# PSUM column order in a hybrid decoder layer: sums kept in the order in which the products read their columns, put back into token order by the evictions

## The chip, the cores and the metric

The kernel runs on one core of one Trainium2 chip. The metric is the device time of one execution in microseconds; the median of several runs is compared. Beside the timed runs there is one profiled execution, whose span is the time from its first to its last instruction.

## What is computed

One decoder layer on 256 tokens and 16 meta tokens, width 2048, all in float32:

```python
h = concatenate([meta, x])                          # 272 tokens
xn = rmsnorm(h, norm_mix_g)
proj = xn @ w_in                                    # fq fk fv ff | gq gk gv gr ga | gate_fox gate_gla
o_fox = forgetting_attention(fq, fk, fv, ff)        # 8 heads of 128
o_gla = gated_linear_attention(gq, gk, gv, g_log)   # 4 heads, keys 256, values 512, chunks of 64
o_gla = head_rmsnorm(o_gla, gla_norm_g) * silu(gr)
y = sigmoid(gate_fox) * (o_fox @ w_o_fox) + sigmoid(gate_gla) * (o_gla @ w_o_gla)
h = h + y @ w_out
h = h + square(relu(rmsnorm(h, norm_mlp_g) @ w_ff1)) @ w_ff2      # 8192 wide
return rmsnorm(h, final_norm_g)[16:]
```

## The kernel before

Everything lies transposed: features on the 128 partitions, tokens along the columns. Each large product makes 128 output features for all tokens at a time, a chunk: its weight block of 2048x128 floats is loaded in two halves of 512 KB on SyncE's queue (`weight_half`, L108), ScalarE rounds a half to the float32r tile whi (L120), and VectorE makes the remainder wlo (L121). The moving operand was split in the same way before, into a high part and a low part that lie beside each other. Five halves of weights are in flight.

Three helpers make the products. `mac2` (L142) multiplies whi by the high and the low part at once, 512 columns (L143), and adds wlo times the high part, 256 columns, to the first half of the bank (L144); so a finished bank holds a main sum in columns 0 to 255 and a sum to be added to it in columns 256 to 511. `mac3` (L146) does the same for the 272 tokens with meta tokens, where a bank has room for 512 columns alone: its three products (L148, L150, L152) are 272 columns wide and overlap in the bank, shifted by 16 columns. `gemm2` (L154) and `gemm_all` (L163) loop over the 16 blocks of the contraction. The first seven chunks are issued interleaved with the input loads (L358 to L376) by matmuls of their own (L364, L366).

All these products read the moving operand in an order of steps: `steps` (L135) cuts the columns into groups of 16, and reads the first 4 of each group, then the next 4 of each group, and so on, in four passes. Before the change the output in PSUM is addressed with the same `steps`, so that each sum lands at its token's own column.

The sums leave PSUM by evictions. `total` (L178) copies columns 256 to 511 with ScalarE (L181) and adds the main sum on VectorE (L184). `join` (L173) folds the last 16 columns of a `mac3` bank into its first 16. `add_residual` (L869) adds both halves of a bank to the residual ht (L872, L873). The 272-column sums are read directly by VectorE: by `keys` (L520) for the GLA keys, and by L603, L722 and L758 for values and attention keys. `keys` makes two outputs of each key bank: kx, four runs of 64 tokens (L524), and kz, the last 16 tokens written four times (L526). The scores of a GLA head (`scores`, L556; matmuls at L562) read kx, qx and kz.

The order of the work on each engine is set by a list scheduler over the recorded program. PSUM has eight banks, three in the pool pg for the large products and five in px for all else. `later(n, fn)` holds a function back until n more chunks are issued.

In the tail, the last four chunks of the second feed-forward product put the wlo products first (L926, 256 columns, in steps) with an eviction of their own (L927), and then the whi products by halves of 128 tokens (L942), which read their tokens in a row and write them in a row.

Of the kernel before, what the change touches and what calls it, by code (L numbers as in the profile page):

```python
# [65 lines left out]
def trunk(ctx: ExitStack, tc: tile.TileContext, hT, w_small, w_all, consts, w_alpha2, out):  # L66
# [3 lines left out]
    def nm(s):  # L70
        serial[0] += 1
        return f"{s}_{serial[0]}"
# [62 lines left out]
    def steps(ap):  # L135

        return ap.rearrange("p (i a e) -> p a i e", a=4, e=4)

    def row(x):
        return x.rearrange("p o t -> p (o t)")  # L140

    def mac2(ps, hi, lo, x, first, last):  # L142
        nc.tensor.matmul(steps(ps), hi, steps(row(x)), start=first, stop=False)  # L143
        nc.tensor.matmul(steps(ps[:, 0:NT]), lo, steps(x[:, 0, :]), start=False, stop=last)  # L144

    def mac3(ps, hi, lo, k, first, last):  # L146
        if hi is not None:
            nc.tensor.matmul(steps(ps[:, X_LO]), hi, steps(x_lo[:, k]), start=first, stop=False, skip_group_check=True)  # L148
        if lo is not None:
            nc.tensor.matmul(steps(ps[:, 0:NA]), lo, steps(x_hi[:, k]), start=False, stop=last and hi is None, skip_group_check=True)  # L150
        if hi is not None:
            nc.tensor.matmul(steps(ps[:, 0:NA]), hi, steps(x_hi[:, k]), start=False, stop=last, skip_group_check=True)  # L152

    def gemm2(w, x, k0=0, nk=KT, pool=None):  # L154

# [16 lines left out]

    def join(ps):  # L173
        b = tmp.tile([P, NM], F32, tag="join", name=nm("join"))
        nc.scalar.copy(b, ps[:, NA : NA + NM])
        nc.vector.tensor_tensor(ps[:, 0:NM], ps[:, 0:NM], b, op=ALU.add)

    def total(ps, t=None):  # L178

        b = tmp.tile([P, NT], F32, tag="evb", name=nm("evb"))  # L180
        nc.scalar.copy(b, ps[:, NT:512])  # L181
        if t is None:
            t = tmp.tile([P, NT], F32, tag="evt", name=nm("evt"), bufs=4)
        nc.vector.tensor_tensor(t, ps[:, 0:NT], b, op=ALU.add)  # L184
        return t

    def split_to(dst_hi, dst_lo, src):
# [145 lines left out]
    for s in range(KT // 2):  # L333
        if s + 3 < KT // 2:
            with tc.issue_after(load_stage(s + 3, 0).ins):
                load_h(nc.sync, 2 * s + 6, 2)
            last = load_stage(s + 3, 1).ins
        wa, wb = stages[s]
        for kk in range(2):
            k = 2 * s + kk  # L340
            nc.scalar.activation(x_hi[:, k], h[:, k, 0:NA], AF.Identity, scale=gain(0, k))
            nc.vector.scalar_tensor_tensor(x_lo[:, k, 0:NT], h[:, k, NM:NA], gain(0, k),
                                           x_hi[:, k, NM:].bitcast(F32), op0=ALU.mult, op1=ALU.subtract)
            xm = meta[:, k, :]
# [12 lines left out]

        def products(c, k, part):  # L358
            hi, lo = at[c][0][:, k % 2, :], at[c][1][:, k % 2, :]
            ps, st, sp = first_ps[c], k == 0, k == KT - 1  # L360
            if c == NF - 1:
                mac3(ps, hi if part == 0 else None, lo if part else None, k, st, sp and part == 1)
            elif part == 0:
                nc.tensor.matmul(steps(ps), hi, steps(row(x[:, k])), start=st, stop=False)  # L364
            else:
                nc.tensor.matmul(steps(ps[:, 0:NT]), lo, steps(x[:, k, 0]), start=False, stop=sp)  # L366
# [141 lines left out]
    def gla_head(hd, sg, ready=None):  # L508
# [9 lines left out]
        Q0, Q3 = Q1 - C, NT - Q1  # L518

        def keys(i, ps):  # L520
            def four(ap):
                return ap.rearrange("p (g s t) -> p g s t", g=2, s=2)

            nc.vector.tensor_tensor(kx[:, i].rearrange("p g (s t) -> p g s t", t=C)[:, :, 0:3:2, :],  # L524
                                    four(ps[:, 0 : 4 * C]), four(en[:, i, 0 : 4 * C]), op=ALU.mult)
            nc.vector.tensor_tensor(kz[:, i], *(ap.unsqueeze(1).to_broadcast([P, 4, NB])  # L526
                                                for ap in (ps[:, 4 * C : NA], en[:, i, 4 * C :])), op=ALU.mult)

        if ready:
            ps = gemm_all(next_weights())  # L530
# [69 lines left out]
        for i in range(4):  # L600
            ps = gemm_all(next_weights())
            vT = tmp.tile([P, NA], F32, tag="vT", name=nm("vT"))
            nc.vector.tensor_tensor(vT, ps[:, 0:NA], rb, op=ALU.mult)  # L603
            nc.gpsimd.tensor_copy(vg[:, NB * i : NB * (i + 1)], vT[:, 4 * C :])
            later(1, lambda i=i, vT=vT: turn(i, vT))

# [60 lines left out]
        w = small[k // HK][:, k % HK, :]  # L667
        mac3(ps, w, None, k, k == 0, k == KT - 1)
    join(ps)
    nc.scalar.copy(both[0:40], ps[64:104, 0:NA])  # L670
    nc.vector.tensor_tensor(both[0:40], ps[0:40, 0:NA], both[0:40], op=ALU.add)
# [46 lines left out]
    def fox_head(hd):  # L718
        fk = att.tile([P, NA], F32, tag="fk", name=nm("fk"))
        fq = att.tile([P, NT], F32, tag="fq", name=nm("fq"))  # L720
        ps = gemm_all(next_weights())
        nc.vector.tensor_tensor(fk, ps[:, 0:NA], rb, op=ALU.mult)  # L722
# [35 lines left out]
        nc.vector.tensor_tensor(vT, ps[:, 0:NA], rb, op=ALU.mult)  # L758
        va, pa = [], []
        vb = att.tile([P, P], F32, tag="vb", name=nm("vb"))  # L760

# [105 lines left out]
            nc.gpsimd.tensor_tensor(acc, acc, sq, op=ALU.add)  # L867

    def add_residual(j, ps):  # L869
        b = tmp.tile([P, NT], F32, tag="evb", name=nm("evb"))  # L870
        nc.scalar.copy(b, ps[:, NT:512])
        nc.vector.tensor_tensor(ht[:, j, :], ps[:, 0:NT], ht[:, j, :], op=ALU.add)  # L872
        nc.vector.tensor_tensor(ht[:, j, :], ht[:, j, :], b, op=ALU.add)  # L873

    acc2 = gat.tile([P, NT], F32, tag="acc", name="acc2", bufs=1)
    for j in range(KT):
# [45 lines left out]
    for n in range(NL):  # L922
        j, ps = KT - NL + n, bank(pg if n < 3 else px, "ps")
        w = next_weights(whi[:, n])
        for k in range(KT):
            nc.tensor.matmul(steps(ps[:, 0:NT]), w(k)[1], steps(a[:, k, 0, :]), start=(k == 0), stop=(k == KT - 1))  # L926
        nc.vector.tensor_tensor(ht[:, j, :], ps[:, 0:NT], ht[:, j, :], op=ALU.add)  # L927
        ends.append((j, w, ps))

    def half(t0, between, within=None):  # L930
# [142 lines left out]
```

## Time and profile before

| | us |
|---|---|
| median of 3 runs | 1567.56 (1567.43 to 1567.89) |
| profiled execution | 1566.89 |
| its span | 1565.1 |
| TensorE matmul busy | 1553.5 |
| VectorE busy | 1060.0 |
| ScalarE busy | 790.4 |
| GpSimd busy | 128.2 |

The granted TensorE clock was 0.999 of full speed throughout. In the rows, PE is TensorE, DVE VectorE, ACT ScalarE, POOL GpSimd. A row in order of time begins with start and duration in us; a waiting row gives in brackets the idle time before it and what ended it. Matmul durations overlap, because one begins before the one before it has left the array; the time from start to start is what one costs. A row of windows gives from:to, the length, and TensorE's busy time with the number of matmuls.

### The profile page before, as it was taken

The numbers are of one execution on the slowest core, as the hardware profiler recorded it, in microseconds if no ns is written. First come the engines' busy times: TensorE is split into PE (matmuls) and PEld (weight loads), VectorE is DVE, ScalarE is ACT, GpSimd is POOL, SyncE is SP. The second block draws the span as 40 slices with busy tenths as digits, with TensorE's granted clock in tenths as the row PEclk, the third lists the DMA queues.
The fourth block names the chain that finished last, engine by engine and source line by source line (L and its number), as shares of the span: only waits on it lengthen the run. The fifth ranks groups of instructions, "written<-read, shape, count | busy, mean of one in ns | idle before, by whom it ended". The sixth has DMA issues, their size and how long they took to land.

```text
span 1565.1 us, 25427 instructions
## 1 busy us (share of the span) xinstructions
PE 1553.5 (99%) x9812; PEld 1408.5 (90%) x9812; DVE 1060.0 (68%) x1659; ACT 790.4 (50%) x1271; POOL 128.2 (8%) x213
## 2 busy tenths in 40 slices
PE   9999999999999999999999999999999999999997
PEld 8999999999998888888888888888888888888887
DVE  7898857676665555555777876567655776567655
ACT  7666444455555444444555444444444444444563
POOL 6012000011100000000011000000000000000022
PEclk9999999999999999999999999999999999999999
DMA  9444545555455555555555555555555555555552
GB/s 325 157 166 158 187 162 182 173 190 172 162 172 183 194 191 193 194 193 189 187 199 192 186 190 196 194 190 193 194 191 190 197 191 195 196 191 197 189 183 104
DMA packets 86602, 293.09 MB, mean 187 GB/s; under 512 B 9112, under 2 KB 16800, under 8 KB 86352
## 3 DMA queue, kind: packets, MB, share of 16 engines
q1 hardware_dynamic: 85872, 289.62, 54.9%
q8 instruction: 77, 1.26, 0.3%
q0 software_dynamic: 176, 1.12, 0.2%
q10 hardware_dynamic: 432, 0.72, 0.1%
q14 instruction: 45, 0.37, 0.1%
HBM read 289.32 MB, written 2.11 MB: 186 GB/s over the span
## 4 chain that ended last, share of the span: by engine, by line
PE 97%; ACT 1%; DVE 1%; issue 0%; DMA 0%; POOL 0%; SPq 0%; POOLq 0%; ACTq 0%; DVEq 0%
PE ps L143 51%; PE ps L144 26%; PE psa L152 4%; PE psa L148 4%; PE psa L150 4%; PE ps L364 1%; PE ps L366 1%; PE ps L942 1%; PE pa L562 1%; PE ps L926 0%; ACT whi L120 0%; DVE wlo L121 0%; DMA raw<-w_all_dram 0%; PE po L625 0%; POOL o L990 0%
## 5 line engine op out<-in xcount | busy, mean ns | idle before, releaser
L121 DVE TENSOR_TENSOR wlo<-raw,whi 128x1024 fp32r<-128x1024 f32 x522 | 640.6, 1227 | 427.9 <-ACT whi L120 426.6
L120 ACT CAST whi<-raw 128x1024 fp32r<-128x1024 f32 x522 | 548.2, 1050 | 633.0 <-PE ps L143 474.6
L143 PE MATMUL ps<-x,whi 128*128 128x512 f32 x1952 | 671.7, 389 | 0.7 <-DVE x L879 0.7
L144 PE MATMUL ps<-x,wlo 128*128 128x256 f32 x1952 | 540.0, 277 | 0.0
L143 PEld LDWEIGHTS ps<-x,whi 128*128 128x128 f32 x1952 | 366.2, 188 | 75.5 <-DVE x L879 1.1
L144 PEld LDWEIGHTS ps<-x,wlo 128*128 128x128 f32 x1952 | 367.3, 188 | 0.1
L143 PE MATMUL ps<-a,whi 128*128 128x512 f32 x960 | 327.3, 387 | 0.0
L144 PE MATMUL ps<-a,wlo 128*128 128x256 f32 x960 | 264.4, 276 | 0.0
L143 PEld LDWEIGHTS ps<-a,whi 128*128 128x128 f32 x960 | 179.6, 187 | 36.4
L148 PE MATMUL psa<-x,whi 128*128 128x272 f32 x640 | 182.3, 286 | 0.0
L144 PEld LDWEIGHTS ps<-a,wlo 128*128 128x128 f32 x960 | 180.7, 188 | 0.3
L152 PE MATMUL psa<-x,whi 128*128 128x272 f32 x640 | 180.6, 283 | 0.0
L150 PE MATMUL psa<-x,wlo 128*128 128x272 f32 x624 | 176.9, 283 | 0.0
L148 PEld LDWEIGHTS psa<-x,whi 128*128 128x128 f32 x640 | 120.4, 188 | 0.3
L152 PEld LDWEIGHTS psa<-x,whi 128*128 128x128 f32 x640 | 120.2, 188 | 0.0
L150 PEld LDWEIGHTS psa<-x,wlo 128*128 128x128 f32 x624 | 117.1, 188 | 0.0
L867 POOL TENSOR_TENSOR acc<-acc,hsq 128x256 f32<-128x256 f32 x26 | 28.9, 1112 | 754.3 <-ACT hsq L866 754.3
L143 PE MATMUL ps<-y,whi 128*128 128x512 f32 x256 | 87.9, 389 | 0.0
L143 PE MATMUL ps<-og,whi 128*128 128x512 f32 x256 | 87.8, 387 | 0.0
L144 PE MATMUL ps<-y,wlo 128*128 128x256 f32 x256 | 70.9, 278 | 0.0
L144 PE MATMUL ps<-og,wlo 128*128 128x256 f32 x256 | 70.5, 275 | 0.0
L184 DVE TENSOR_TENSOR evt<-ps,evb 128x256 f32<-128x256 f32 x158 | 65.7, 417 | 0.5 <-ACT evb L181 0.5
(297 smaller groups left out, 1420.8 us busy)
## 6 DMA issues: line engine op xcount, KB each, us to landing
raw<-w_all_dram SPq DMA_DIRECT2D x537, 512.0 KB, 3.7
raw<-w_all_dram SPq DMA_DIRECT2D x8, 384.0 KB, 6.6
h<-hT_dram SPq DMA_DIRECT2D x8, 275.0 KB, 6.6
negc<-fdram POOLq DMA_DIRECT2D x1, 1088.0 KB, 7.7
out_dram<-o SPq DMA_DIRECT2D x2, 512.0 KB, 2.6
raw<-w_all_dram SPq DMA_DIRECT2D x2, 256.0 KB, 3.8
room<-w_small_dram SPq DMA_DIRECT2D x1, 320.0 KB, 7.7
out_dram<-o ACTq DMA_DIRECT2D x1, 320.0 KB, 3.1
```

Of the source, the lines that this page charges most:

```text
L120: nc.scalar.copy(hi[:, k, :], r)
L121: nc.vector.tensor_tensor(lo[:, k, :], r, hi[:, k, :].bitcast(F32), op=ALU.subtract)
L143: nc.tensor.matmul(steps(ps), hi, steps(row(x)), start=first, stop=False)
L144: nc.tensor.matmul(steps(ps[:, 0:NT]), lo, steps(x[:, 0, :]), start=False, stop=last)
L148: nc.tensor.matmul(steps(ps[:, X_LO]), hi, steps(x_lo[:, k]), start=first, stop=False, skip_group_check=True)
L150: nc.tensor.matmul(steps(ps[:, 0:NA]), lo, steps(x_hi[:, k]), start=False, stop=last and hi is None, skip_group_check=True)
L152: nc.tensor.matmul(steps(ps[:, 0:NA]), hi, steps(x_hi[:, k]), start=False, stop=last, skip_group_check=True)
L184: nc.vector.tensor_tensor(t, ps[:, 0:NT], b, op=ALU.add)
L364: nc.tensor.matmul(steps(ps), hi, steps(row(x[:, k])), start=st, stop=False)
L366: nc.tensor.matmul(steps(ps[:, 0:NT]), lo, steps(x[:, k, 0]), start=False, stop=sp)
L562: nc.tensor.matmul(dst, k[:, a], q[:, a, :], start=(a == 0), stop=(a == 1))
L867: nc.gpsimd.tensor_tensor(acc, acc, sq, op=ALU.add)
```

## The change

The large products write PSUM in the order in which they read: `mac2`'s 512-column product fills the bank from column 0 to 511 in a row, and a 256-column product fills four runs of 64 columns, the first half of each run of 128. In `mac3`, the bank is seen as four runs of 72 columns, and the three products fill 68 columns of each, shifted by 4. What was at a token's column is now at the place of its pass. The evictions read PSUM through the new views `read` and `in_order` and so bring the columns back into token order.

```diff
+    def read(ps, n):
+        return ps[:, 0 : 16 * n].rearrange("p (a i e) -> p a i e", a=4, e=4)
+    def in_order(ps):
+        return ps[:, 0:288].rearrange("p (a i e) -> p i a e", a=4, e=4)
+    def rows16(ap):
+        return ap.rearrange("p (i a e) -> p i a e", a=4, e=4)
...
     def mac2(ps, hi, lo, x, first, last):
-        nc.tensor.matmul(steps(ps), hi, steps(row(x)), start=first, stop=False)
-        nc.tensor.matmul(steps(ps[:, 0:NT]), lo, steps(x[:, 0, :]), start=False, stop=last)
+        nc.tensor.matmul(ps, hi, steps(row(x)), start=first, stop=False)
+        nc.tensor.matmul(read(ps, 32)[:, :, 0:16], lo, steps(x[:, 0, :]), start=False, stop=last)
...
     def mac3(ps, hi, lo, k, first, last):
+        above, below = read(ps, 18)[:, :, 0:17], read(ps, 18)[:, :, 1:18]
-            nc.tensor.matmul(steps(ps[:, X_LO]), hi, steps(x_lo[:, k]), start=first, ...)
+            nc.tensor.matmul(below, hi, steps(x_lo[:, k]), start=first, ...)
...
     def join(ps):
-        nc.scalar.copy(b, ps[:, NA : NA + NM])
-        nc.vector.tensor_tensor(ps[:, 0:NM], ps[:, 0:NM], b, op=ALU.add)
+        b = b.rearrange("p (a e) -> p a e", e=4)
+        meta, rest = in_order(ps)[:, 0], in_order(ps)[:, 17]
+        nc.scalar.copy(b, rest)
+        nc.vector.tensor_tensor(meta, meta, b, op=ALU.add)
+    def lower_sum(ps):
+        b = tmp.tile([P, NT], F32, tag="evb", name=nm("evb"))
+        nc.scalar.copy(b.rearrange("p (a c) -> p a c", a=4), ps.rearrange("p (a c) -> p a c", a=4)[:, :, 64:])
+        return read(b, 16)
     def total(ps, t=None):
-        nc.scalar.copy(b, ps[:, NT:512])
+        b = lower_sum(ps)
-        nc.vector.tensor_tensor(t, ps[:, 0:NT], b, op=ALU.add)
+        nc.vector.tensor_tensor(steps(t), read(ps, 32)[:, :, 0:16], b, op=ALU.add)
...
         def keys(i, ps):
-            nc.vector.tensor_tensor(kx[:, i].rearrange("p g (s t) -> p g s t", t=C)[:, :, 0:3:2, :],
-                                    four(ps[:, 0 : 4 * C]), four(en[:, i, 0 : 4 * C]), op=ALU.mult)
-            nc.vector.tensor_tensor(kz[:, i], *(ap.unsqueeze(1).to_broadcast([P, 4, NB])
-                                                for ap in (ps[:, 4 * C : NA], en[:, i, 4 * C :])), op=ALU.mult)
+            src = in_order(ps)
+            for g in range(2):
+                for s in range(2):
+                    at = 2 * g + s
+                    nc.vector.tensor_tensor(rows16(kx[:, i, g, 2 * s * C : (2 * s + 1) * C]),
+                                            src[:, 4 * at : 4 * at + 4],
+                                            rows16(en[:, i, at * C : (at + 1) * C]), op=ALU.mult)
+            nc.vector.tensor_tensor(kz[:, i, 0, :].rearrange("p (a e) -> p a e", e=4), src[:, 16],
+                                    en[:, i, 4 * C :].rearrange("p (a e) -> p a e", e=4), op=ALU.mult)
+            nc.gpsimd.tensor_copy(kz[:, i, 1:4, :], kz[:, i, 0:1, :].to_broadcast([P, 3, NB]))
...
-            nc.vector.tensor_tensor(vT, ps[:, 0:NA], rb, op=ALU.mult)
+            nc.vector.tensor_tensor(rows16(vT), in_order(ps)[:, 0:17], rows16(rb), op=ALU.mult)
...
     def add_residual(j, ps):
-        nc.scalar.copy(b, ps[:, NT:512])
-        nc.vector.tensor_tensor(ht[:, j, :], ps[:, 0:NT], ht[:, j, :], op=ALU.add)
-        nc.vector.tensor_tensor(ht[:, j, :], ht[:, j, :], b, op=ALU.add)
+        b, to = lower_sum(ps), steps(ht[:, j, :])
+        nc.vector.tensor_tensor(to, read(ps, 32)[:, :, 0:16], to, op=ALU.add)
+        nc.vector.tensor_tensor(to, to, b, op=ALU.add)
```

The other two products of `mac3`, the first chunks' matmuls, the wlo products of the tail with their eviction, the attention keys and values, and the forget gate's sums are changed in the same manner. The moving operands are read as before.

On TensorE, in the interleaved first chunks (ps_85 to ps_91 are their seven banks, x the operand, whi and wlo the weights; the last numbers are the output's shape, partitions first), before the change:

```order
L364 MATMUL ps_89<-x,whi_113 128x4x32x4
L364 MATMUL ps_90<-x,whi_113 128x4x32x4
L148 MATMUL ps_91<-x,whi_113 128x4x17x4
L152 MATMUL ps_91<-x,whi_113 128x4x17x4
L366 MATMUL ps_85<-x,wlo_110 128x4x16x4
```

The same place now:

```order
L382 MATMUL ps_89<-x,whi_113 128x512
L382 MATMUL ps_90<-x,whi_113 128x512
L160 MATMUL ps_91<-x,whi_113 128x4x68
L164 MATMUL ps_91<-x,whi_113 128x4x68
L384 MATMUL ps_85<-x,wlo_110 128x4x64
```

Nothing moved there; the output of the 512-column product is now one run, and those of the narrower ones are four. The later chunks, written by `mac2` and `mac3`, have the same shapes. On VectorE, at the keys of GLA head 0 (qx and kx are the decayed queries and keys, wlo the next weights), before:

```order
L121 TENSOR_TENSOR wlo_1181<-raw_1179,whi_1180 128x1024
L524 TENSOR_TENSOR kx_662<-ps_91,en_all 128x2x2x64
L526 TENSOR_TENSOR kz_663<-ps_91,en_all 128x64
L524 TENSOR_TENSOR kx_662<-psa_677,en_all 128x2x2x64
L526 TENSOR_TENSOR kz_663<-psa_677,en_all 128x64
L432 TENSOR_TENSOR room<-room 128x544
```

VectorE at the same place now:

```order
L121 TENSOR_TENSOR wlo_1193<-raw_1191,whi_1192 128x1024
L543 TENSOR_TENSOR kx_662<-ps_91,en_all 128x64 x4
L546 TENSOR_TENSOR kz_663<-ps_91,en_all 128x16
L543 TENSOR_TENSOR kx_662<-psa_677,en_all 128x64 x4
L546 TENSOR_TENSOR kz_663<-psa_677,en_all 128x16
L450 TENSOR_TENSOR room<-room 128x544
```

Two instructions a call became five, at the same place; a GpSimd copy for each call is added. On TensorE, the first scores of the same head (pa is their bank) stand among the products of a later chunk (psa); before:

```order
L152 MATMUL psa_1111<-x,whi_1106 128x4x17x4
L562 MATMUL pa_1002<-qx_664,kx_662 64x48
L148 MATMUL psa_1111<-x,whi_1106 128x4x17x4
L150 MATMUL psa_1111<-x,wlo_1107 128x4x17x4
L562 MATMUL pa_1002<-qx_664,kx_662 64x48
L562 MATMUL pa_1002<-qx_664,kx_662 64x64 x2
L562 MATMUL pa_1002<-qx_664,kz_663 64x16 x2
```

TensorE at the same place now:

```order
L583 MATMUL pa_1010<-qx_664,kx_662 64x48
L164 MATMUL psa_1119<-x,whi_1114 128x4x68
L160 MATMUL psa_1119<-x,whi_1114 128x4x68
L162 MATMUL psa_1119<-x,wlo_1115 128x4x68
L583 MATMUL pa_1010<-qx_664,kx_662 64x48
L583 MATMUL pa_1010<-qx_664,kx_662 64x64 x2
L583 MATMUL pa_1010<-qx_664,kz_663 64x16 x2
```

The first score moved ahead of one product; the last two rows of scores, with kz, stand where they stood.

More of the change, by code (lines that the diff above doesn't have):

```diff
@@ L142, in mac2 @@
     def mac2(ps, hi, lo, x, first, last):
[L143 to L144 removed]
+        nc.tensor.matmul(ps, hi, steps(row(x)), start=first, stop=False)
+        nc.tensor.matmul(read(ps, 32)[:, :, 0:16], lo, steps(x[:, 0, :]), start=False, stop=last)
     def mac3(ps, hi, lo, k, first, last):
+        above, below = read(ps, 18)[:, :, 0:17], read(ps, 18)[:, :, 1:18]
         if hi is not None:
[L148 removed]
+            nc.tensor.matmul(below, hi, steps(x_lo[:, k]), start=first, stop=False, skip_group_check=True)
         if lo is not None:
[L150 removed]
+            nc.tensor.matmul(above, lo, steps(x_hi[:, k]), start=False, stop=last and hi is None, skip_group_check=True)
         if hi is not None:
[L152 removed]
+            nc.tensor.matmul(above, hi, steps(x_hi[:, k]), start=False, stop=last, skip_group_check=True)
     def gemm2(w, x, k0=0, nk=KT, pool=None):
@@ L363, in products @@
             elif part == 0:
-                nc.tensor.matmul(steps(ps), hi, steps(row(x[:, k])), start=st, stop=False)
+                nc.tensor.matmul(ps, hi, steps(row(x[:, k])), start=st, stop=False)
             else:
-                nc.tensor.matmul(steps(ps[:, 0:NT]), lo, steps(x[:, k, 0]), start=False, stop=sp)
+                nc.tensor.matmul(read(ps, 32)[:, :, 0:16], lo, steps(x[:, k, 0]), start=False, stop=sp)
         if s < KT // 2 - 1:
@@ L669, in trunk @@
     join(ps)
-    nc.scalar.copy(both[0:40], ps[64:104, 0:NA])
-    nc.vector.tensor_tensor(both[0:40], ps[0:40, 0:NA], both[0:40], op=ALU.add)
+    nc.scalar.copy(rows16(both[0:40]), in_order(ps)[64:104, 0:17])
+    nc.vector.tensor_tensor(rows16(both[0:40]), in_order(ps)[0:40, 0:17], rows16(both[0:40]), op=ALU.add)
     nc.vector.tensor_tensor(both[0:40], both[0:40], rb[0:40], op=ALU.mult)
@@ L721, in fox_head @@
         ps = gemm_all(next_weights())
[L722 removed]
+        nc.vector.tensor_tensor(rows16(fk), in_order(ps)[:, 0:17], rows16(rb), op=ALU.mult)
         t = total(gemm2(next_weights(), x))
@@ L925, in trunk @@
         for k in range(KT):
-            nc.tensor.matmul(steps(ps[:, 0:NT]), w(k)[1], steps(a[:, k, 0, :]), start=(k == 0), stop=(k == KT - 1))
-        nc.vector.tensor_tensor(ht[:, j, :], ps[:, 0:NT], ht[:, j, :], op=ALU.add)
+            nc.tensor.matmul(ps[:, 0:NT], w(k)[1], steps(a[:, k, 0, :]), start=(k == 0), stop=(k == KT - 1))
+        nc.vector.tensor_tensor(steps(ht[:, j, :]), read(ps, 16), steps(ht[:, j, :]), op=ALU.add)
         ends.append((j, w, ps))
```

6 lines of the change are left out of this document (1 added, 5 removed).

## The prediction

> **What bounds the kernel now.** I read the page first, then the waits of TensorE, then rows in order of time where the change adds something.
>
> ```profile
> span 1565.1 us, 25427 instructions
> PE 1553.5 (99%) x9812; PEld 1408.5 (90%) x9812; DVE 1060.0 (68%) x1659; ACT 790.4 (50%) x1271; POOL 128.2 (8%) x213
> PE 97%; ACT 1%; DVE 1%; issue 0%; DMA 0%; POOL 0%; SPq 0%; POOLq 0%; ACTq 0%; DVEq 0%
> PE ps L143 51%; PE ps L144 26%; PE psa L152 4%; PE psa L148 4%; PE psa L150 4%; PE ps L364 1%; PE ps L366 1%; PE ps L942 1%; PE pa L562 1%; PE ps L926 0%; ACT whi L120 0%; DVE wlo L121 0%; DMA raw<-w_all_dram 0%; PE po L625 0%; POOL o L990 0%
> ```
>
> TensorE is 97% of the chain that ended last, and the products whose PSUM order changes (L143 to L152, L364, L366) are 91%, 1424 us: the product stream is the kernel. The question is therefore whether a product gets shorter, and whether anything new makes TensorE stand still. It hardly ever stands still now; these are all its listed waits:
>
> ```profile
> PE warm L328 <- DVE ones L208: 1.3, 1, 1.3
> PE ps L143 <- DVE x L879: 0.7, 1, 0.7
> PE ps L364 <- ACT whi L293: 0.7, 2, 0.4
> PE pn L966 <- ACT sq L947: 0.7, 1, 0.7
> PE pa L562 <- DVE kx L524: 0.5, 1, 0.5
> ```
>
> Together 3.9 us. No eviction appears among them: nowhere does TensorE wait for a PSUM bank to be read out. One of the five, 0.5 us at the first scores of GLA head 0, is behind exactly the function that the change rewrites.
>
> **The products.** The durations in the page overlap (a 512-column product is listed at 389 ns), so a price must come from counts over time. Two feed-forward stages, slowest and fastest, with window, busy time and number of matmuls:
>
> ```profile
> 1118.00:1205.00 87.00, 87.00 (x509) 1.00 0.56 191
> 1293.00:1380.00 87.00, 87.00 (x516) 1.00 0.57 195
> ```
>
> A product costs 87.00/509 = 170.9 ns in the one and 87.00/516 = 168.6 ns in the other. Half are 512 columns wide (L143) and half 256 (L144), 384 on average: 0.4451 and 0.4391 ns per column. I take their mean, 0.442. All of them write PSUM in steps: 4 columns, then a jump of 16.
>
> What would a product cost that writes PSUM in a row? The trace has some, in the tail: L942 reads and writes rows of 128 columns, L926 beside it reads and writes in steps, both 256 columns wide. The chain there:
>
> ```profile
> 1533.15 5.53 PE ps L926 x48
> 1538.67 1.62 PE ps L942 x14
> 1540.29 0.91 PE ps L926 x8
> 1542.34 7.28 PE ps L942 x64
> ```
>
> Stepped: 5.53/48 = 115.2 ns and 0.91/8 = 113.8 ns. In a row: 1.62/14 = 115.7 and 7.28/64 = 113.8 ns. The two kinds cover the same interval, 0.444 to 0.450 against 0.444 to 0.452 ns per column. Furthermore, a step occurs every 4 columns, 64 times in a 256-column product. If a step cost anything, single stepped products could not be as short as neighbours show:
>
> ```profile
> 1299.77 0.27 PE L144 MATMUL ps<-a,wlo 128*128 128x256 f32 x1
> 1299.88 0.38 PE L143 MATMUL ps<-a,whi 128*128 128x512 f32 x1
> 1300.10 0.28 PE L144 MATMUL ps<-a,wlo 128*128 128x256 f32 x1
> ```
>
> From start to start 0.11 us for 256 stepped columns, 0.22 for 512: below the 113.8 ns of the row-writing kind. So the value I take for the change in the product rate is **zero**. The moving operand is read in the same steps after the change as before, so what varies a product by its operand's place stays. The bounds from both sides, over the chain's 1424 us: if row writing is worth L942's 0.444 against L926's 0.450 ns, -1.3% or **-19 us**; if every product came to the dearest row-writing rows, 0.452 against the mean of 0.442, +2.3% or **+32 us**.
>
> [...]
>
> **The evictions.** Their number stays but for the keys; their access becomes stepped on the PSUM side and, in `total` and `add_residual`, on the SBUF side. The profile's group rows for contiguous ones:
>
> ```profile
> L184 DVE TENSOR_TENSOR evt<-ps,evb 128x256 f32<-128x256 f32 x158 | 65.7, 417 | 0.5 <-ACT evb L181 0.5
> L181 ACT COPY evb<-ps 128x256 f32<-128x256 f32 x160 | 58.3, 365 | 1.3 <-DVE evt L184 0.9 <-PE ps L366 0.3
> L524 DVE TENSOR_TENSOR kx<-psa,en_all 128x256 f32<-128x256 f32 x7 | 2.9, 416 | 0.0
> ```
>
> L524 already moves 256 columns in runs of 64 with gaps on its output, at 416 ns against 417 in one run, so gaps between runs cost nothing there. Runs of 4 the trace does not show. I take no price; the upper bound is a doubling, +0.42 us an eviction (below nothing there is no room, since no operand shrinks). Even so doubled it is covered: a chunk of 32 products lasts 32 x 170 ns = 5.4 us, VectorE is 68% busy, and three banks of pg stand between eviction and reuse. Where that cover is thin is the first 100 us, which comes next. Before the late stall (0.7 us for L879) stands this:
>
> ```profile
> 857.92 0.43 DVE L873 TENSOR_TENSOR h<-h,evb 128x256 f32<-128x256 f32 x1
> 859.05 1.23 DVE L121 TENSOR_TENSOR wlo<-raw,whi 128x1024 fp32r<-128x1024 f32 x1 [0.70 <-ACT whi L120]
> ```
>
> The eviction's last add is followed by 0.70 us in which VectorE waits for a weight cast of ScalarE; a few tenths more fit there. In the tail the evictions of L926's products lie beside the 7.28 us of L942.
>
> **The keys, where the path is touched.** VectorE's rows at head 0 now:
>
> ```profile
> 82.73 1.22 DVE L121 TENSOR_TENSOR wlo<-raw,whi 128x1024 fp32r<-128x1024 f32 x1
> 83.86 0.42 DVE L524 TENSOR_TENSOR kx<-ps,en_all 128x256 f32<-128x256 f32 x1
> 84.19 0.21 DVE L526 TENSOR_TENSOR kz<-ps,en_all 128x64 f32<-128x64 f32 x1
> 84.33 0.41 DVE L524 TENSOR_TENSOR kx<-psa,en_all 128x256 f32<-128x256 f32 x1
> 84.66 0.21 DVE L526 TENSOR_TENSOR kz<-psa,en_all 128x64 f32<-128x64 f32 x1
> 84.79 0.71 DVE L432 TENSOR_TENSOR room<-room 128x544 f32<-128x544 f32 x1
> ```
>
> By starts, one call of `keys` takes 0.33 + 0.14 = 0.47 us. After the change it is four multiplies of 64 columns, at L526's 0.14 each, and one of 16, about 0.10: 0.66 us, +0.19 a call. The last kz is then written near 83.86 + 1.32 + 0.1 = 85.25 instead of 84.87. TensorE now:
>
> ```profile
> 84.33 0.32 PE L562 MATMUL pa<-qx,kx 128*64 128x48 f32 x2 [0.51 <-DVE kx L524]
> 85.02 0.56 PE L562 MATMUL pa<-qx,kx 128*64 128x48 f32 x6
> 85.41 0.36 PE L562 MATMUL pa<-qx,kz 128*64 128x16 f32 x4
> 85.70 0.39 PE L152 MATMUL psa<-x,whi 128*128 128x272 f32 x1
> ```
>
> The first score can start some 0.2 us earlier, because it needs only the first quarter of kx. The kz score at 85.41 is another matter: it now also needs the second copy on GpSimd. A GpSimd copy's price is in these rows:
>
> ```profile
> 78.23 1.20 POOL L604 COPY vg<-vT 128x16 f32<-128x16 f32 x1 [3.80 <-DVE ends L441]
> 82.87 1.14 POOL L548 COPY qx<-qx 128x32 f32<-128x32 f32 x1 [3.44 <-DVE qx L539]
> L770 POOL COPY vg<-vT 128x16 f32<-128x16 f32 x16 | 2.8, 205 | 96.2 <-DVE vT L758 91.6 <-PE pu L810 4.7
> ```
>
> It is 0.2 us undisturbed, but the copy of 82.87 ended at 84.01, just after the L121 of 82.73 (83.95): it stood still until VectorE's two-input instruction was through. Ready at 85.25, the second kz copy meets the room multiply (0.71 us, then at 85.2) and ends at about 86.1, or behind the next L121 at about 87.4. TensorE would reach the kz score near 85.2, so the new wait is 0.9 to 2.2 us; less the 0.2 gained, +0.7 to +2.0. I take **+1.0 us**, near the case of the room multiply. Behind that score stand all further products, in program order, so TensorE's loss is the kernel's. In heads 1 to 3 the scores run much later than the keys; for head 1, the last key row and the chain's row of the scores:
>
> ```profile
> 97.33 0.21 DVE L526 TENSOR_TENSOR kz<-psa,en_all 128x64 f32<-128x64 f32 x1
> 127.34 2.11 PE pa L562 x20
> ```
>
> Thirty us cover the copies and the extra 0.4 us of VectorE per head; should that cover go, each head would cost the same +1 us.
>
> **Sum.** Profiled execution 1566.89 us (span 1565.1) + 0 (products) + 0 (evictions) + 1.0 (head 0) = 1567.9. The median shown, 1567.56, is 0.67 above that execution, so the forecast for the median is **1568.6 us**.
>
> **Rivals.**
> - *Row writing is quicker.* [...] Against it: L926's own x8 at 113.8, and single stepped products at 110. It gives 1568.6 - 19 = 1549.6.
> - *Head 0 becomes a real stall* (the other side). The mechanism is TensorE's queue behind the second kz copy. If reads in runs of 4 cost double, the ten multiplies take 2.6 rather than 1.3 us, the copy becomes ready at 86.6 and falls behind the L121 after the room multiply, to about 88.7 where TensorE stands since 85.2: a wait of 3.5, less 0.2, or 1567.56 + 3.3 = 1570.9. It decides from a net loss of 3.1 us up. For it: the rows above, where VectorE has no gap from 82.73 on. Against it: L524's runs cost nothing.
> - *Row writing is dearer*: 0.452 against 0.442 ns, 1568.6 + 32 = 1600.6. For it only the 14 products at 115.7 ns; against it the 64 at 113.8.
> - That the change does not do what it says is excluded: the program's rows show 128x512 outputs in place of 128x4x32x4.
>
> **How the numbers follow.** Forecast 0.55, quicker writing 0.18, head 0 stall 0.17, dearer writing 0.10. A measurement of this kernel can tell about 0.2% (3.1 us) from no change. Inside the forecast the stages' own spread (0.4391 to 0.4451 about 0.442, 10 us each way if the rhythm shifts everywhere) can carry it out on either side, 0.05 and 0.07. Faster: 0.18 + 0.05 = 0.23. Slower: 0.07 + 0.14 (most of the stall) + 0.10 = 0.31. Same: 0.46. The range 1550 to 1578 holds the forecast with that spread, the stall and half of the quicker case; left out are 0.09 below and 0.10 above. The forecast's own range is 1558 to 1578.
>
> **What would show it.** The stage windows: matmuls in 87 us stay at 509 to 516; 520 and more speaks for quicker writing, 500 and less for dearer. The waits of TensorE: a new line for kz on GpSimd of 1 to 2 us, the one for kx at 0.3 to 0.6. The evictions stay at about 417 and 365 ns; 0.6 us and more would say that runs of 4 cost. Wrong would be any product rate that moves by over 0.5% with the operand reads unchanged.

## The result and the profile after

The changed kernel takes 1567.67 us in the median of 12 runs (1567.23 to 1568.29), the kernel before 1567.45 us beside it (12 runs, 1566.95 to 1568.27): a ratio of 1.0001 with an interval of 0.9992 to 1.0010. That is no difference that the measurement can tell, 0.9 us under the forecast. The profiled execution took 1567.33 us, its span is 1565.5 us against 1565.1.

The product stages first. The same two feed-forward windows as before, in the changed kernel (from:to and length; busy time and number of instructions of TensorE, of its weight loads, of VectorE, ScalarE and GpSimd; then clock, DMA share and GB/s):

```profile
1118.00:1205.00 87.00, 87.00 (x509) 77.11 (x508) 51.90 (x67) 38.25 (x49) 0.00 (x0) 1.00 0.58 191
1293.00:1380.00 87.00, 87.00 (x516) 77.68 (x516) 53.03 (x68) 38.22 (x49) 0.00 (x0) 1.00 0.58 195
```

509 and 516 products, the counts of before to the last one. Each operand keeps its own pace, too: in the trace a pair of products (512 and 256 columns, from start to start) of the operand y (of the product with `w_out`) takes 343.3 ns before and after, of the four a (of the second feed-forward product) 341.1, 343.3, 338.5 and 341.4 ns before and after.

All waits of TensorE in the changed kernel:

```profile
PE warm L346 <- DVE ones L226: 1.3, 1, 1.3
PE ps L154 <- DVE x L899: 0.8, 1, 0.8
PE pn L986 <- ACT sq L967: 0.7, 1, 0.7
PE pa L583 <- POOL kz L548: 0.6, 1, 0.6
PE ps L382 <- ACT whi L311: 0.6, 1, 0.6
PE pa L583 <- DVE kx L543: 0.3, 1, 0.3
```

The fourth row is new: the scores of head 0 wait for kz on GpSimd, once, 0.6 us. The last row was 0.5 us before. The others are the old ones at their new lines, within 0.1 us.

The evictions, as groups (count, busy time, mean ns of one), first three of the kernel before, then those of the changed kernel:

```profile
L872 DVE TENSOR_TENSOR h<-ps,h 128x256 f32<-128x256 f32 x76 | 31.7, 418 | 3.9 <-ACT evb L871 3.9
L873 DVE TENSOR_TENSOR h<-h,evb 128x256 f32<-128x256 f32 x76 | 32.4, 426 | 2.5
L603 DVE TENSOR_TENSOR vT<-psa,rb 128x272 f32<-128x272 f32 x16 | 7.0, 435 | 0.5
```

```profile
L202 DVE TENSOR_TENSOR evt<-ps,evb 128x256 f32<-128x256 f32 x158 | 65.9, 418 | 0.5 <-ACT evb L194 0.5
L892 DVE TENSOR_TENSOR h<-ps,h 128x256 f32<-128x256 f32 x76 | 32.6, 428 | 3.6 <-ACT evb L194 3.6
L893 DVE TENSOR_TENSOR h<-h,evb 128x256 f32<-128x256 f32 x76 | 33.3, 439 | 2.5
L194 ACT COPY evb<-ps 128x256 f32<-128x256 f32 x236 | 86.2, 366 | 1.3 <-PE ps L384 1.3
L624 DVE TENSOR_TENSOR vT<-psa,rb 128x272 f32<-128x272 f32 x16 | 7.0, 437 | 0.5
```

The reads of PSUM in runs of 4 columns are those through `in_order`: L624 takes 437 ns for 272 columns against 435 in a row, and the attention keys and values (L743, L779) 441 against 440. The reads through `read` and `lower_sum` take PSUM in four runs of 64 columns: 418 ns against 417 in L202, which writes SBUF in steps of 4, and 366 against 365 in L194. Only L892 and L893, which also read SBUF in steps of 4, went from 418 and 426 ns to 428 and 439.

VectorE and then TensorE and GpSimd at head 0, where the change touches the path:

```profile
83.90 0.61 DVE L543 TENSOR_TENSOR kx<-ps,en_all 128x64 f32<-128x64 f32 x4
84.43 0.16 DVE L546 TENSOR_TENSOR kz<-ps,en_all 128x16 f32<-128x16 f32 x1
84.51 0.60 DVE L543 TENSOR_TENSOR kx<-psa,en_all 128x64 f32<-128x64 f32 x4
85.04 0.16 DVE L546 TENSOR_TENSOR kz<-psa,en_all 128x16 f32<-128x16 f32 x1
85.12 0.71 DVE L450 TENSOR_TENSOR room<-room 128x544 f32<-128x544 f32 x1
```

```profile
84.17 0.32 PE L583 MATMUL pa<-qx,kx 128*64 128x48 f32 x2 [0.27 <-DVE kx L543]
...
85.37 0.24 PE L583 MATMUL pa<-qx,kz 128*64 128x16 f32 x2
86.21 0.29 PE L583 MATMUL pa<-qx,kz 128*64 128x16 f32 x2 [0.60 <-POOL kz L548]
86.43 0.39 PE L164 MATMUL psa<-x,whi 128*128 128x272 f32 x1
```

```profile
84.66 0.22 POOL L548 COPY kz<-kz 128x48 f32<-128x48 f32 x1 [0.60 <-DVE kz L546]
85.26 0.90 POOL L548 COPY kz<-kz 128x48 f32<-128x48 f32 x1 [0.38 <-DVE kz L546]
```

The first copy takes 0.22 us, beside the kx multiplies of 84.51. The second meets the room multiply (85.12 to 85.83) and two multiplies of qx behind it (85.75 to 86.20), takes 0.90 us and ends at 86.16, and TensorE goes on at 86.21. The next product starts at 86.43; before, the same product started at 85.70, 0.73 us earlier.

### The profile page after: what moved, and what is told of

Read it like the earlier page. It is cut to its first block, busy times and chain, and to the rows that moved or that the text cites. A ratio compares the mean times of both kernels' runs of the same rounds, so it can differ in the third digit from the quotient of the medians.

```text
span 1565.5 us, 25477 instructions
## 1 busy us (share of the span) xinstructions
PE 1553.7 (99%) x9812; PEld 1408.4 (90%) x9812; DVE 1063.9 (68%) x1683; ACT 790.5 (50%) x1271; POOL 136.9 (9%) x221
## 4 chain that ended last, share of the span: by engine, by line
PE 96%; DVE 1%; ACT 1%; issue 0%; DMA 0%; POOL 0%; SPq 0%; POOLq 0%; DVEq 0%; ACTq 0%
PE ps L154 51%; PE ps L155 26%; PE psa L164 4%; PE psa L160 4%; PE psa L162 4%; PE ps L382 1%; PE ps L962 1%; PE ps L384 1%; PE pa L583 0%; PE ps L946 0%; DMA raw<-w_all_dram 0%; DVE wlo L121 0%; ACT whi L120 0%; PE po L646 0%; POOL o L1010 0%
## 5 line engine op out<-in xcount | busy, mean ns | idle before, releaser
L194 ACT COPY evb<-ps 128x256 f32<-128x256 f32 x236 | 86.2, 366 | 1.3 <-PE ps L384 1.3
```

The lines of the kernel that those rows point to most:

```text
L194: nc.scalar.copy(b.rearrange("p (a c) -> p a c", a=4), ps.rearrange("p (a c) -> p a c", a=4)[:, :, 64:])
```

## The experiments

**Theory:** what a product costs is set by the order and the place in which it reads its moving operand. Where its sums land in PSUM is free, in the old order and in the new, and the evictions lie under the products. **Rivals:** writing costs something too, but runs of 4 columns are still long enough to hide it, and shorter runs would show it; or two effects cancel, a quicker product against the new wait; or the evictions are near the bound and only just fit.

### Shorter runs in PSUM

In the changed kernel the two products of `mac2` write PSUM in runs of two columns; reads and evictions stay. The sums of these chunks land at other tokens.

```diff
+    def pairs(ps):
+        return ps.rearrange("p (f a i g) -> p a i f g", f=2, a=4, g=2)
     def mac2(ps, hi, lo, x, first, last):
-        nc.tensor.matmul(ps, hi, steps(row(x)), start=first, stop=False)
-        nc.tensor.matmul(read(ps, 32)[:, :, 0:16], lo, steps(x[:, 0, :]), start=False, stop=last)
+        nc.tensor.matmul(pairs(ps), hi, steps(row(x)), start=first, stop=False)
+        nc.tensor.matmul(pairs(ps[:, 0:NT]), lo, steps(x[:, 0, :]), start=False, stop=last)
```

> All mac2 products write PSUM in runs of 2 columns with a jump behind each, in place of one run of 512 or four of 64 (the evictions are those of the change, so sums land at other tokens' columns: the output is not the reference's). Theory, the write order costs a product nothing as long as it writes whole pairs: within 0.2% of before (1564.5 to 1570.7 us), 509 to 516 matmuls in an 87 us window of the feed-forward stages as before. Rival, a jump costs something that shows only with short runs: at one column's time a jump (0.44 ns), 256 + 128 jumps make a pair 341 + 169 = 510 ns, +600 us over 3552 pairs; at a tenth of that still +60 us.

Measured: 1567.70 us (10 runs, 1567.03 to 1568.54), a ratio of 0.9999 (0.9989 to 1.0009). Windows of 86 us, first with runs of two and then in the changed kernel:

```profile
957.00:1043.00 86.00, 86.00 (x506) 76.13 (x505) 52.14 (x66) 37.03 (x48) 0.00 (x0) 1.00 0.61 198
1139.00:1225.00 86.00, 86.00 (x503) 76.18 (x502) 51.58 (x66) 38.03 (x50) 0.00 (x0) 1.00 0.59 192
```

```profile
957.00:1043.00 86.00, 86.00 (x506) 76.12 (x505) 51.67 (x66) 37.51 (x48) 0.00 (x0) 1.00 0.58 197
1139.00:1225.00 86.00, 86.00 (x504) 76.22 (x504) 52.16 (x66) 37.56 (x50) 0.00 (x0) 1.00 0.58 193
```

506 against 506, 503 against 504. Runs of two columns, of four (the kernel before), of 64 and of 512 all cost the same. Runs of one column were not measured.

One stage moves by more than one product: the third of x2 (the operand of the first feed-forward product), 1206 to 1293 us, has 514 in the kernel before and in the changed one, and 512 with pairs. The writes are not the reason, for the run with kz on VectorE, further down, writes as the changed kernel does and has 511. The changed kernel, then that run:

```profile
1206.00:1293.00 87.00, 87.00 (x514) 77.19 (x513) 62.43 (x94) 42.53 (x63) 0.00 (x0) 1.00 0.57 194
1206.00:1293.00 87.00, 87.00 (x511) 77.07 (x510) 62.08 (x94) 42.48 (x63) 0.00 (x0) 1.00 0.60 192
```

In the first, every pair of the stage takes 339 or 340 ns; in the second and with runs of two columns, pairs go up and down between 330 and 355 ns and take 341.4 on average. So the same reads at the same place can run in two rhythms, 0.4% apart. What chooses between them was not found.

### The order of reading and of writing, one at a time

In the kernel before, `row_row` reads and writes in a row (`steps` becomes the identity, for the 272-column products as well):

```diff
     def steps(ap):
-        return ap.rearrange("p (i a e) -> p a i e", a=4, e=4)
+        return ap
```

> The kernel before with reads and writes of all large products in a row (no steps on either side). Theory, the order of the reads sets the rate of a product and the order of the writes does not: the rate becomes that of the tail's row-reading products, 0.444 to 0.452 ns per column against a mean of 0.442, so 1574 to 1600 us, slower than before. Rival, no order matters on either side: 1566 to 1569 us and 509 to 516 matmuls per 87 us window, as before.

`row_steps` reads in a row and writes in steps, in `mac2` and the first chunks; the evictions gather the sums from there:

```diff
+    def half2(ap):
+        return ap.rearrange("p (a i e) -> p a i e", a=2, e=4)
     def mac2(ps, hi, lo, x, first, last):
-        nc.tensor.matmul(steps(ps), hi, steps(row(x)), start=first, stop=False)
-        nc.tensor.matmul(steps(ps[:, 0:NT]), lo, steps(x[:, 0, :]), start=False, stop=last)
+        nc.tensor.matmul(steps(ps), hi, row(x), start=first, stop=False)
+        nc.tensor.matmul(steps(ps)[:, 0:2], lo, x[:, 0, :], start=False, stop=last)
```

> The kernel before with mac2 products (and the first chunks) reading in a row but still writing PSUM in steps, evictions adapted; the 272-column products as before. Theory (writes are free): the feed-forward windows show the same count as those of row_row within 2 matmuls, whatever that is; the time lies between before and row_row. Rival, it is the match of read and write order that counts: the windows differ from row_row's by 1% (5 matmuls) or more.

Measured: `row_row` 1605.99 us (4 runs, 1605.74 to 1606.19), ratio 1.0243 (1.0228 to 1.0258); `row_steps` 1598.47 us (4 runs, 1597.51 to 1599.38), ratio 1.0195 (1.0180 to 1.0210). Windows of `row_row`, then of `row_steps`:

```profile
300.00:480.00 180.00, 180.00 (x1290) 171.49 (x1289) 119.02 (x239) 90.83 (x191) 21.82 (x60) 1.00 0.52 169
957.00:1043.00 86.00, 86.00 (x489) 75.33 (x488) 51.23 (x69) 37.17 (x49) 0.00 (x0) 1.00 0.57 185
1139.00:1225.00 86.00, 86.00 (x497) 75.43 (x496) 51.39 (x67) 37.39 (x50) 0.00 (x0) 1.00 0.58 190
```

```profile
300.00:480.00 180.00, 180.00 (x1303) 170.81 (x1303) 120.72 (x242) 94.48 (x197) 22.51 (x61) 1.00 0.53 173
957.00:1043.00 86.00, 86.00 (x488) 75.28 (x488) 50.14 (x65) 36.76 (x48) 0.00 (x0) 1.00 0.57 187
1139.00:1225.00 86.00, 86.00 (x497) 75.42 (x496) 50.38 (x65) 37.21 (x48) 0.00 (x0) 1.00 0.58 189
```

Reading in a row drops the feed-forward windows from the 506 and 504 of the kernel before to 488 to 497, whichever way the sums are written: from y on, a pair of products takes 346.7 to 353.4 ns in both kernels against 338.5 to 343.3 with steps. Writing in steps or in a row makes 488 against 489, and stage by stage the pairs of the two kernels agree to 0.1 ns. The kernels part where the 272-column products run (300 to 480 us, 1303 against 1290), because only `row_row` reads those in a row too: 1605.99 - 1598.47 = 7.5 us over 1952 such products, 3.9 ns each. The direction was as expected; `row_row` came out somewhat dearer than the range given for it.

### Longer jumps in reading

In the kernel before, `mac2` reads and writes in eight passes, so that the jump is 32 columns instead of 16:

```diff
+    def steps8(ap):
+        return ap.rearrange("p (i a e) -> p a i e", a=8, e=4)
     def mac2(ps, hi, lo, x, first, last):
-        nc.tensor.matmul(steps(ps), hi, steps(row(x)), start=first, stop=False)
-        nc.tensor.matmul(steps(ps[:, 0:NT]), lo, steps(x[:, 0, :]), start=False, stop=last)
+        nc.tensor.matmul(steps8(ps), hi, steps8(row(x)), start=first, stop=False)
+        nc.tensor.matmul(steps8(ps[:, 0:NT]), lo, steps8(x[:, 0, :]), start=False, stop=last)
```

> The kernel before with the mac2 products read and written in steps of another width: 4 columns, then a jump of 32 in place of 16 (eight passes). Theory, the read order sets the rate and the write order does not: the pairs change by 1 to 4% in one direction, and jumps of 32 are at most as quick as jumps of 16: 1567 to 1600 us. Rival, only reading in a row is special and all steps are alike: windows within 2 matmuls of before, 1566 to 1569 us.

Measured: 1645.77 us (4 runs, 1645.31 to 1646.23), ratio 1.0500 (1.0486 to 1.0514). Two of its windows:

```profile
943.00:1030.00 87.00, 87.00 (x486) 74.18 (x485) 54.38 (x77) 38.66 (x55) 0.00 (x0) 1.00 0.57 183
1206.00:1293.00 87.00, 87.00 (x475) 74.35 (x474) 50.28 (x66) 36.15 (x49) 0.00 (x0) 1.00 0.55 180
```

A pair takes 360 to 369 ns. The order of reading does set the rate, but the size was missed by far: jumps of 32 columns are dearer than no jumps at all, while jumps of 16 are cheaper. Here, too, order and place are not all: the second stage of x2 takes 360.0 ns a pair and the third 366.7, with the same operand at the same place.

### Double work on the evictions

In the changed kernel the add in `total` is issued twice:

```diff
         nc.vector.tensor_tensor(steps(t), read(ps, 32)[:, :, 0:16], b, op=ALU.add)
+        nc.vector.tensor_tensor(steps(t), read(ps, 32)[:, :, 0:16], b, op=ALU.add)
```

> The changed kernel with the VectorE add of every total eviction issued twice (158 to 160 more adds of 0.42 us, by starts 0.33; same result). Theory, evictions are covered by the product stream: VectorE busy +66 us, time within 0.2% of before. Rival, evictions stand on the path: 160 x 0.33 = +53 us, 1620 us; half of it if only the stages with a busy VectorE count.

Measured: 1572.72 us (5 runs, 1572.49 to 1575.31), ratio 1.0036 (1.0023 to 1.0049), outside the 0.2% expected. VectorE has 160 instructions more and its busy time grew from 1063.9 to 1112.8 us; 5.1 us came through to the time, a tenth of these 48.9. The feed-forward stages are untouched (957 to 1043 us: x506 as before). The waits of TensorE for VectorE that are new or longer, in order of time:

```profile
88.91 0.32 PE L584 MATMUL pa<-qx,kx 128*64 128x48 f32 x2 [2.25 <-DVE kx L544]
89.51 0.59 PE L584 MATMUL pa<-qx,kx 128*64 128x48 f32 x6 [0.29 <-DVE kx L544]
```

```profile
766.78 0.47 PE L154 MATMUL ps<-og,whi 128*128 128x512 f32 x1 [0.66 <-DVE evt L203]
```

3.2 us stand in these waits. Two are at head 0, 2.54 us against 0.87 in the changed kernel; the third is in the last chunks of og (the operand of the GLA output product), where the row names the doubled add. The first twenty scores of head 1 start at 131.63 us against 127.81 in the changed kernel, and those of head 3 at 279.55 against 275.69, so 3.8 us (3.86 at head 3) were lost by head 1 and no more up to head 3. The waits at head 0 are 1.7 of them. About as much went another way: behind the stall the granted clock of TensorE fell. The changed kernel, then the run with the doubled add:

```profile
90.00:94.00 4.00, 4.00 (x35) 4.00 (x34) 4.00 (x10) 2.23 (x9) 1.34 (x2) 1.00 0.47 159
90.00:94.00 4.00, 4.00 (x23) 3.97 (x22) 4.00 (x11) 0.00 (x0) 1.58 (x2) 0.57 0.51 171
```

A product of 272 columns took 227 ns there, against some 123 at full clock; over the stretch that is some 1.6 us. The cover is real for nine tenths of the work, and missing at head 0 and once at og. The rival by which all of it comes through is refuted.

### kz without GpSimd

In the changed kernel VectorE makes the three further copies of kz in place of GpSimd.

```diff
-            nc.gpsimd.tensor_copy(kz[:, i, 1:4, :], kz[:, i, 0:1, :].to_broadcast([P, 3, NB]))
+            nc.vector.tensor_copy(kz[:, i, 1:4, :], kz[:, i, 0:1, :].to_broadcast([P, 3, NB]))
```

> The changed kernel with the three further copies of kz made by VectorE in place of GpSimd. Theory, TensorE's 0.60 us at the second kz score is GpSimd standing behind VectorE's two-input instruction: the wait for kz on GpSimd is gone, what is left at that score is at most 0.2 us, and the time is 0 to 0.6 us below the changed kernel, 1567.1 to 1567.7 (hardly to be told from it by time, so the wait is the measure). Rival, the score would have waited anyway for VectorE's own keys: a wait of 0.4 us or more remains there, named after DVE.

Measured: 1567.76 us (11 runs, 1567.25 to 1568.81), ratio 1.0003 (0.9994 to 1.0012). The waits of TensorE, all of them:

```profile
PE warm L346 <- DVE ones L226: 1.3, 1, 1.3
PE ps L154 <- DVE x L899: 0.8, 1, 0.8
PE pn L986 <- ACT sq L967: 0.7, 1, 0.7
PE ps L946 <- DVE h L892: 0.3, 1, 0.3
PE pa L583 <- DVE kx L543: 0.3, 1, 0.3
```

The row of kz on GpSimd is gone. But more than the engine changed: the scheduler now puts the two copies at 87.29 and 87.73 us, where GpSimd made them at 84.66 and 85.26, and the kz scores at 88.23 and 88.89, among later products, where nothing makes them wait. So this run does not show what the copy costs on VectorE at the old place. That the wait was the copy's is told by the rows of the changed kernel: VectorE had finished the last kz at 85.20, TensorE was idle from 85.61, the copy ended at 86.16 and TensorE went on at 86.21. VectorE's own keys, the rival of this run, were done before TensorE came. The time is the same to what can be measured, which says that the wait is worth little, and cannot say more: 0.6 us is less than the interval. That no quicker product hides behind the wait is told by the unchanged windows of the changed kernel, and with them the rival of two effects that cancel falls.

### The place of the operand

If the place of reading sets the rate, the spread between the stages can be had as a gain. The fastest stage before and after is the third a, whose tile begins 48 columns in. `at48` gives that place to y and all four a in the changed kernel, `at48b` to x2 as well:

```diff
-    y = operand(keep, "y", at=4, tag="s1")
+    y = operand(keep, "y", at=48, tag="s1")
...
-        a = operand(keep, "a", at=(0, 4, 48, 0)[g], tag="s1")
+        a = operand(keep, "a", at=48, tag="s1")
```

> The changed kernel with y and all four feed-forward operands a at an offset of 48 columns in their tile, as only the third a has it. Theory, with the write order free, what is left of a product's rate is the place of its moving operand: all second feed-forward stages show 516 matmuls per 87 us as the third does (509 to 512 before), the y stage too (509 before), about 2.8 ns a pair over 256 + 192 pairs and 4.8 over 512: -3.5 to -4 us, 1563.7 to 1564.2. Rival, the rate goes with what stands around the stage (weights, banks, evictions): no stage moves by over 1 matmul, 1567.2 to 1568.

> As at48, and x2, the operand of the first feed-forward product, at an offset of 48 columns too (0 before). Theory: its four stages go from 341 to about 338.5 ns a pair as well, 1024 pairs by 2.5 ns: a further -2.5 us, 1561 to 1562 in all. Rival (place does not matter, or matters only for a): the same as at48 within 0.5 us.

Measured: `at48` 1564.91 us (11 runs, 1564.30 to 1566.49), ratio 0.9985 (0.9976 to 0.9993); `at48b` 1561.59 us (5 runs, 1561.03 to 1562.90), ratio 0.9966 (0.9952 to 0.9979). Windows of `at48`, one of an operand a and one of x2, and then the same windows of `at48b`:

```profile
943.00:1030.00 87.00, 87.00 (x517) 77.70 (x516) 52.83 (x68) 38.63 (x51) 0.00 (x0) 1.00 0.59 195
1206.00:1293.00 87.00, 87.00 (x512) 77.03 (x511) 62.79 (x94) 42.09 (x64) 0.00 (x0) 1.00 0.60 193
```

```profile
943.00:1030.00 87.00, 87.00 (x516) 77.70 (x516) 52.63 (x67) 38.61 (x51) 0.00 (x0) 1.00 0.60 195
1206.00:1293.00 87.00, 87.00 (x515) 77.70 (x515) 63.60 (x96) 42.81 (x64) 0.00 (x0) 1.00 0.60 195
```

The stages of y, a and x2 whose operand moved all go to the 515 to 517 of the third a. Those of x2 in `at48`, where it had not moved, have 511 or 512, the third of them in the slower of its two rhythms. The gain of `at48`, 2.8 us beside the kernel before, is smaller than the 3.5 to 4 expected; that of `at48b`, 6.1 us, is as expected. In the profiled execution of `at48`, its longest with 1566.49 us, the clock fell to 0.50 from 87 to 90 us, behind a wait of 0.66 us for kz: between the score that waits and the next scores 5.61 us passed, 4.04 in `at48b`, some 1.6 us that have nothing to do with the place. `at48b` waited 0.66 us there, too, and kept its clock.

### The same place with the old writes

The last run asks whether that gain needs the new order of writing. It is the kernel before, with its stepped writes and its evictions, and with og, y, x2 and the a at 48:

```diff
-            og_box.append(operand(keep, "og", at=0, tag="s2"))
+            og_box.append(operand(keep, "og", at=48, tag="s2"))
```

> The kernel before with its old stepped PSUM writes and old evictions; only the operands og, y, x2 and the four of the second feed-forward product begin 48 columns into their tiles. Theory (a product's cost is set by the order and place in which it reads its operand; where its sum lands in PSUM is free): the stages run at 338.3 to 338.6 ns per pair of products as with the changed kernel's writes, x515 to x517 in 87 us in every feed-forward stage, and the 256 pairs of og gain 256 x 2.6 ns = 0.7 us more, so 1567.5 - 6.0 - 0.7 = 1560.8, between 1560.0 and 1562.0. Rival (the place of reading and the order of writing act together, so that the gain needs the writes in reading order): the stages stay at their former counts in some windows, x509 to x514, and the time is 1563 or more.

Measured: 1561.03 us (5 runs, 1560.81 to 1561.22), ratio 0.9960 (0.9946 to 0.9973). Its windows:

```profile
943.00:1030.00 87.00, 87.00 (x516) 77.74 (x515) 52.39 (x67) 38.48 (x51) 0.00 (x0) 1.00 0.59 196
1206.00:1293.00 87.00, 87.00 (x516) 77.70 (x515) 63.55 (x96) 42.78 (x64) 0.00 (x0) 1.00 0.60 195
```

From y on the rates are those of `at48b` to within 0.2 ns a pair, with the other order of writing, so the gain does not need the new one. Both versions beat both kernels, by 6.1 and 6.5 us against the runs of before beside them. Only og gave less than expected: its pairs went from 341.4 to 339.9 ns, not to 338.3 to 338.6, which is 0.4 us instead of 0.7.

## Why the prediction was right, point by point

- **The products: zero.** Right, and for the reason given, as far as it rests on averages. The three single products shown as shorter than any that writes in a row were a lucky pick: in that stage the 256-column products go from 109 to 121 ns, 113.9 on average, so they do not lie below 113.8. The counts of the windows stayed, and the runs with pairs in PSUM, with rows read and steps written, and with the old writes at the new place show in three ways that the write order does not enter. The tail, which carried the rival of quicker writing, gives no such sign any more: the products of 256 columns that wrote in steps at 115.2 and 113.8 ns now take 5.50/48 = 114.6 and 0.91/8 = 113.8. The chain's row of the last 64 products (whose code did not change) in the changed kernel, and then in the one with kz on VectorE:

```profile
1542.54 7.54 PE ps L962 x64
```

```profile
1543.85 7.28 PE ps L962 x64
```

  117.8 ns in the one and 113.8 in the other, as before the change, with the same operands and the same writes. So a few ns here belong to neither order; what they belong to was not found.
- **The length of the runs in PSUM.** Runs of two columns take 1567.70 us, runs of 512 and 64 take 1567.67, and runs of 4, in the kernel before, 1567.45. Nothing here goes below two.
- **The evictions: zero.** Right in the sum. Reading PSUM in runs of 4 costs 1 or 2 ns in some 440, and in runs of 64 it costs 1 ns in 417; `total` and `add_residual` read PSUM in runs of 64 only, so the price of runs of 4 that the prediction bounded for them falls on the keys and values alone. The SBUF side, which it did not price apart, costs 10 to 13 ns in `add_residual`, where it is also read in steps, and is covered. The argument that the evictions would be covered even if doubled was too strong: doubling one of their adds cost 5.1 us, at head 0, where the prediction itself called the cover thin, with a fall of the clock behind the stall, and at og, which it did not name.
- **The keys.** The call takes 84.51 - 83.90 = 0.61 us, where 0.66 was worked out.
- **The wait for kz: mis-sized.** The kind was right: a new wait on GpSimd, the second copy held up (by the times in the rows) beside the room multiply and the two of qx behind it, and not behind the next weight remainder, its end at 86.16 where 86.1 was said. That a VectorE instruction has two inputs is not enough for that: the first copy took 0.22 us beside the kx multiplies, which have two as well. Which instructions hold a copy up was not asked. The size was 0.60 us, not 0.9 to 2.2. The prediction let all four kz scores stand behind the second copy. Two of them need only the first and ran at 85.37, so TensorE arrived later at the one that waits. Less the 0.24 us gained at kx, the waits grew by 0.36, where +0.7 to +2.0 was said and +1.0 taken. The time cannot tell the one from the other: the medians differ by 0.2 us, and +1.0 would have lain within the interval as well. That the forecast came within 0.9 us of the time says nothing for this term.
- **What came back.** From the next product's start (0.73 us late at 86.43) the lag shrinks to 0.18 us at the scores of 201 us, where the scheduler had put the small products of heads 0 and 1 into another order; it is 0.18 still at 1533.33 us, and the tail's last 64 products with their 0.26 us make it the 0.4 of the span. That the other order is what gave the half microsecond back is argued, not shown. `at48b` and `at48` run the same program as the changed kernel up to there, and start the scores of head 1 at 127.70 and, with the fall of the clock, at 129.83 us, where the changed kernel has 127.81: a few tenths in one trace are a thin measure.
- **The rivals.** Head 0 as a real stall would have needed reads in runs of 4 at double cost; they took 437 ns against 435 for 272 columns. Dearer writing has no window that speaks for it.

## What to carry to other kernels

This change of PSUM layout was worth what it did to the evictions and to the waits, not to the products: with float32r products of 256 to 512 columns, runs of two columns gave 1567.70 us and runs of 64 and 512 gave 1567.67; shorter runs were not measured. Ask first whether the operand is read in another order or at another place. Where stages of equal work run at different rates (here 509 to 516 products in 87 us), look for what differs in their operands' place and try that of the fastest for every stage. Work beside the bound was free only where it had slack (of 48.9 us of doubled adds 5.1 came through): judge the first stage by itself, look at the clock behind a stall as well as at the stall (some 1.6 us beside 1.7 at head 0), and count for every waiting product which of the writes it really needs. And where a scheduler orders the work, an experiment that moves an instruction to another engine can move it in time, too: read the rows before the time.

## What the runs showed of the hardware

- The order and place in which TensorE reads its moving operand from SBUF change its rate by up to 9%, at a mean granted clock of 0.997 to 0.999. Per pair of float32r products (512 and 256 columns, a new weight block each, from y on): in a row 346.7 ns with the operand at column 4 or 48 of its tile and 350.0 to 353.4 at column 0; in runs of 4 with jumps of 16 columns 340.0 to 341.4 ns at column 0, 343.3 at 4 and 338.3 to 338.7 at 48 (og, before y, 339.9 at 48); with jumps of 32 columns 360 to 369 ns. They are not all that sets it: the same reads at the same place took 340.0 and 341.4 ns in two runs, and 360.0 and 366.7 in two stages of one run. Why is open.
- A short stall cost more than its length in two executions. Behind 2.54 us of waits at head 0 (the doubled add) TensorE's mean granted clock was 0.57 from 90 to 94 us, 1.00 in the changed kernel, and a product of 272 columns took 227 ns in place of some 123. In `at48`, behind 0.66 us, the clock fell to 0.50 from 87 to 90 us, and from the score that waits to the next scores it took 5.61 us. Behind 0.60 us in the changed kernel, and behind the same 0.66 with runs of two columns and in `at48b`, the clock stayed at 1.00, and that stretch took 3.96, 4.05 and 4.04 us. What decides was not found.
- VectorE read PSUM in runs of 4 floats at 437 ns for 272 columns, against 435 in a row; an add that reads SBUF in such runs went from 426 to 439 ns for 256 columns.
- A GpSimd copy of 48 columns took 0.22 us beside four VectorE multiplies of 64 columns that read PSUM, and 0.90 us beside a VectorE multiply of 544 columns in SBUF, which took 0.71 us, and the two of 128 columns behind it.
